# Forgetting attention: the third PSUM bank of the turned probabilities taken from another pool

## Chip, cores, metric

One Trainium2 chip, one of its cores. The metric is the device time of one execution in microseconds; the kernel before is given by the median of three runs. Every reading of the profile comes from one further, profiled execution.

The engines are called as in the profile: PE (TensorE, matrix products; PEld is its weight load), DVE (VectorE), ACT (ScalarE), POOL (GpSimd) and SP (SyncE, which only issues DMAs here). PE writes to PSUM, a memory of eight banks, each of 512 float32 values on each of 128 partitions; ACT and DVE read it from there.

## What is computed

One layer of a streaming encoder on 512 frames of 1024 channels, in float32. A combined projection of the normalised input feeds three branches: gated linear attention (GLA), forgetting attention with eight heads of 64 channels, and cross attention into 256 memory tokens. They are merged by gates, and a squared-ReLU MLP follows. The change lies in the forgetting attention:

```python
def forgetting_attention(q, k, v, log_f):
    F = jnp.cumsum(log_f, axis=1).transpose(0, 2, 1)
    ...
        s = jnp.einsum('bhqd,bhkd->bhqk', qi, kh) * scale
        s = s + Fi[..., None] - F[:, :, None, :]
        mask = k_pos[None, :] <= q_pos[:, None]
        p = jax.nn.softmax(jnp.where(mask, s, -jnp.inf), axis=-1)
        return jnp.einsum('bhqk,bhkd->bhqd', p.astype(vh.dtype), vh)
```

## The kernel before

**Precision and staging.** A float32 product is made of two or three reduced-precision ones: each operand is split into a high part (an ACT cast, `hi`, `PTh`, `whi`) and a low part (a DVE subtraction, `lo`, `PTl`, `wlo`), by `split` (L208 and L209) or `split_w` (L145 and L146), and `mm3` (L155 to L157) multiplies the parts. Weights come in chunks of 512 KB by SP's queue into `raw`, are split, and feed a projection `gT` (eight units of three matmuls of 512 columns, into one PSUM tile, which its `evac` empties).

**PSUM.** Two pools share the eight banks, four each. `mmt()` takes a tile of the pool `pmm`, meant for projections; `at_()` takes one of `pa`, meant for the attention steps. A tile's bank is free when the last instruction that reads the tile is done; the first matmul into the next tile of that bank waits for this.

**Order of the work.** PE's instructions run in the order in which the program text issues them. The order on the other engines is set at compile time by a scheduler that simulates the program; every engine runs its own list strictly in order.

**The stage of the change.** For each head h there are three steps:

- `fox_scores(h)`: adds the causal mask to a row of decays `nFb` (L515; `nFb` is fetched by a DMA from ACT's queue, L506), then for four query tiles takes a bank with `at_()`, makes two matmuls (L526, L527) of 256, 256, 384 and 512 columns, and empties the bank by one DVE instruction (L530), which also finds the row maximum; exponent (ACT, L532), reciprocal (L534) and scaling (L535) follow in `Pt`.
- `fox_turn(h)`: turns the lower triangle of the probabilities, ten blocks of 128 x 128, by PE transposes into three banks: `b0` (four blocks, L542), `b1` (four, L544 and L546) and `b2` (two, L549). Each bank is emptied by a split into `PTh` (ACT) and `PTl` (DVE): 512, 512 and 256 columns.
- `fox_values(h)`: takes one bank `po`, multiplies with the values (L558, L559), and adds the two halves of `po` (ACT copy `th` L563, DVE `oT` L567). After each odd head the pair's output is split into `ofh` and `ofl`.

`weave` strings these together as `fox_values(h-2)`, `fox_turn(h-1)`, `fox_scores(h)` for h from 1 to 9, as far as they exist, and puts units of projections in between, so that PE has work while ACT and DVE do the softmax. The 96 units are, in this order, `gla_k(0)` (8), `fox_pair(2)` (Q, then K: 16), `gla_k(1)` (8), `fox_pair(3)` (16), `gla_q(0)` and `gla_q(1)` (16), and the GLA values `gvg` (32). `gvg` opens four `pmm` tiles at once and holds them to the end of the stage. By the shares in `weave`, `fox_turn(0)` comes behind the end of the K projection of pair 1, `fox_turn(2)` one unit after the K projection of pair 2, `fox_turn(4)` two units after that of pair 3; `fox_turn(5)` comes at unit 62, two ahead of `gvg`.

A K projection is emptied by `k_evac` in two halves of 64 partitions: each an ACT cast and a DVE subtraction out of PSUM (`K`, L208 and L209) and an ACT copy to the other partitions (L497). A Q projection is emptied by `q_evac` in two halves (L490, L491 with the tile `tq`, L492).

So a head takes eight tiles of `pa`: one for `po`, three for the turn, four for the scores.

Of the kernel before, what the change touches and what calls it, by code (L numbers as in the profile page):

```python
# [64 lines left out]
def hybrid_block(ctx, tc, chunks, wst, memT, xN, cols, gffn, gfin, wup, cst, out):  # L65
# [6 lines left out]
    def nm(s):  # L72
        uid[0] += 1
        return f"{s}_{uid[0]}"
# [10 lines left out]
    def mmt(shape=None):  # L85
        return pmm.tile(shape or [P, 512], F32, tag="mm", name=nm("mm"))

    def at_(shape=None):
        return pa.tile(shape or [P, 512], F32, tag="a", name=nm("a"))
# [117 lines left out]
    def split(hi, lo, src):  # L207
        nc.scalar.copy(hi, src)  # L208
        return nc.vector.tensor_tensor(lo, src, f(hi), op=ALU.subtract).ins  # L209
# [41 lines left out]
    with pool("front") as fp:  # L251
# [101 lines left out]
        for k in range(KT):  # L353
# [3 lines left out]
            if k in (3, 5):  # L357
                h = k // 5
# [42 lines left out]
    with pool("fox") as xp:  # L401
# [135 lines left out]

        def fox_turn(h):
            Ps = live.pop(h)
            b0, b1, b2 = at_(), at_(), at_()  # L540
            for i in range(NT):
                nc.tensor.transpose(b0[:, i * P:(i + 1) * P], Ps[i][:, 0:P], ident)  # L542
            split(PTh[:, 0:512], PTl[:, 0:512], b0)
            nc.tensor.transpose(b1[:, 0:P], Ps[3][:, 3 * P:], ident)  # L544
            for i in range(1, NT):
                nc.tensor.transpose(b1[:, i * P:(i + 1) * P], Ps[i][:, P:2 * P], ident)  # L546
            split(PTh[:, 640:1152], PTl[:, 640:1152], b1)
            for i in range(2, NT):
                nc.tensor.transpose(b2[:, (i - 2) * P:(i - 1) * P], Ps[i][:, 2 * P:3 * P], ident)  # L549
            split(PTh[:, 1152:1408], PTl[:, 1152:1408], b2[:, :256])  # L550
# [53 lines left out]
        for h in range(1, 10):  # L604
            for fn, i, n in ((fox_values, h - 2, 3), (fox_turn, h - 1, 2), (fox_scores, h, 3)):
                if 0 <= i < 8:
                    steps.append(partial(fn, i))
                    shares.append(n)
# [882 lines left out]
```

## Time and profile before

| | us |
|---|---|
| median of 3 runs | 828.68 |
| lowest and highest | 828.56, 829.0 |
| the profiled execution's own time | 828.11 |
| its span, from the first to the last instruction | 826.3 |
| ACT busy in the span | 457.9 |
| POOL busy in the span | 104.8 |
| the forgetting attention's score matmuls (L526), first and last start | 77.1, 168.7 |

A row of the timeline or of the groups has start, duration, engine, line, operation, the tile written and the tiles read, and shapes. "[0.66 <-DVE PTl L209]" says that the engine was idle for 0.66 us ahead of this instruction, and that DVE's instruction at L209, which writes `PTl`, ended the wait. "x3" is three instructions in one row, whose duration runs from the start of the first to the end of the last. Successive instructions on one engine can overlap by a fraction, so PE's progress is read from the starts: two full projection matmuls start 0.23 us apart, though each is shown as 0.39 us long. Rows of stretches give start and end, length, and for each engine the busy time with the number of instructions, then the granted clock of PE, the DMA engines' busy share and GB/s. Rows of waits give the waiting engine, tile and line, what it waited for, the total in us, how often, and the longest.

### The profile page before, as it was taken

The page shows a single profiled execution, that of the slowest core. Times are in us where ns is not written, and L with a number is a line of the kernel's source. Part 1 is how long each engine was busy: PE and PEld are TensorE (multiplying, and loading weights), DVE is VectorE, ACT ScalarE, POOL GpSimd, SP SyncE. Part 2 cuts the span into 40 slices and gives each one's busy share as a digit, 9 for nine tenths or more (in the row PEclk, how much of TensorE's full clock was granted, in tenths as well). Part 3 has the DMA queues.
Part 4 walks back from the last instruction along what each step waited for, and adds up shares of the span by engine and source line. Part 5 has one row for each costly group of instructions (what it writes and reads, how often), then busy time and mean ns, then how long its engine had stood idle before and what let it go on. Part 6 is the DMA issues. An engine that isn't in the chain of part 4 may idle for free.

```text
span 826.3 us, 12441 instructions
## 1 busy us (share of the span) xinstructions
PE 813.3 (98%) x4759; PEld 715.4 (87%) x4759; DVE 603.3 (73%) x946; ACT 457.9 (55%) x717; POOL 104.8 (13%) x129
## 2 busy tenths in 40 slices
PE   8999999999999999999999999999999999999996
PEld 6788888888888888989999889988998899889984
DVE  5856887667545686885585647897689778887896
ACT  7765776653345233544354436774577367637764
POOL 1001100101102020132231100011001100110011
PEclk9999999999999999999999999999999999999999
DMA  9525666689687875677676513978757875896644
GB/s 331 183 102 162 185 191 192 190 209 297 146 264 230 229 223 157 128 185 190 151 200 171 178 51 112 275 171 207 237 197 155 229 228 170 191 235 205 164 81 129
DMA packets 39180, 155.60 MB, mean 188 GB/s; under 512 B 4880, under 2 KB 5840, under 8 KB 37072
## 3 DMA queue, kind: packets, MB, share of 16 engines
q1 hardware_dynamic: 27712, 95.54, 33.3%
q0 software_dynamic: 9328, 54.01, 31.7%
q10 hardware_dynamic: 2080, 5.26, 1.8%
q8 instruction: 37, 0.61, 0.3%
q14 instruction: 23, 0.19, 0.1%
HBM read 152.65 MB, written 31.49 MB: 223 GB/s over the span
## 4 chain that ended last, share of the span: by engine, by line
PE 91%; DVE 4%; DMA 2%; issue 1%; ACT 1%; POOL 0%; ACTq 0%; POOLq 0%; DVEq 0%
PE mm L155 23%; PE mm L156 23%; PE mm L157 23%; PE a L156 5%; PE a L155 5%; PE a L157 5%; PE a L797 1%; DMA xn<-in_xN_dram 1%; DMA memr<-in_memT_dram 1%; PE a L526 1%; PE a L559 1%; DVE wlo L146 1%; DVE h L1151 1%; PE a L558 1%; PE a L527 0%
## 5 line engine op out<-in xcount | busy, mean ns | idle before, releaser
L155 PE MATMUL mm<-uhi,whi 128*128 128x512 f32 (+1 forms) x352 | 126.1, 358 | 0.0
L157 PE MATMUL mm<-uhi,wlo 128*128 128x512 f32 (+1 forms) x352 | 123.8, 352 | 0.0
L156 PE MATMUL mm<-ulo,whi 128*128 128x512 f32 (+1 forms) x352 | 123.6, 351 | 0.0
L146 DVE TENSOR_TENSOR wlo<-raw,whi 128x1024 fp32r<-128x1024 f32 x68 | 88.0, 1298 | 43.3 <-ACT whi L145 42.9
L145 ACT CAST whi<-raw 128x1024 fp32r<-128x1024 f32 x68 | 71.3, 1049 | 78.9 <-PE mm L156 45.4
L1155 ACT CAST hi<-raw 128x1024 fp32r<-128x1024 f32 x65 | 68.2, 1049 | 49.6 <-PE mm L156 34.4
L1157 DVE TENSOR_TENSOR lo<-raw,hi 128x1024 fp32r<-128x1024 f32 x65 | 79.6, 1224 | 17.4 <-ACT hi L1155 17.4
L157 PEld LDWEIGHTS mm<-uhi,wlo 128*128 128x128 f32 x352 | 66.6, 189 | 9.1
L155 PEld LDWEIGHTS mm<-uhi,whi 128*128 128x128 f32 x352 | 66.7, 189 | 8.3 <-issue 0.3
L156 PEld LDWEIGHTS mm<-ulo,whi 128*128 128x128 f32 x352 | 66.7, 190 | 8.0
L1155 ACT CAST hi<-b 128x1024 fp32r<-128x1024 f32 x40 | 41.9, 1048 | 42.0 <-PE mm L157 24.0
L156 PE MATMUL mm<-u2l,hi 128*128 128x256 f32 x224 | 63.4, 283 | 0.0
L157 PE MATMUL mm<-u2h,lo 128*128 128x256 f32 x224 | 63.4, 283 | 0.0
L155 PE MATMUL mm<-u2h,hi 128*128 128x256 f32 x224 | 63.4, 283 | 0.0
L1341 POOL DMA_DIRECT2D b<-in_wst_dram x32 | 27.3, 853 | 271.3 <-DVE lo L1157 199.9
L1157 DVE TENSOR_TENSOR lo<-b,hi 128x1024 fp32r<-128x1024 f32 x40 | 48.9, 1224 | 14.1 <-ACT hi L1155 13.9
L156 PE MATMUL mm<-lo,ch 128*128 128x512 f32 x136 | 52.9, 389 | 0.0
L157 PE MATMUL mm<-hi,cl 128*128 128x512 f32 x136 | 52.9, 389 | 0.0
L155 PE MATMUL mm<-hi,ch 128*128 128x512 f32 x136 | 52.9, 389 | 0.0
L156 PE MATMUL mm<-u2sl,hi 128*128 128x256 f32 x168 | 47.6, 283 | 0.0
L157 PE MATMUL mm<-u2sh,lo 128*128 128x256 f32 x168 | 47.6, 283 | 0.0
L155 PE MATMUL mm<-u2sh,hi 128*128 128x256 f32 x168 | 47.6, 283 | 0.0
(401 smaller groups left out, 2159.9 us busy)
## 6 DMA issues: line engine op xcount, KB each, us to landing
raw<-in_wst_dram SPq DMA_DIRECT2D x114, 512.0 KB
b<-in_wst_dram POOLq DMA_DIRECT2D x32, 512.0 KB, 5.5
raw<-T SPq DMA_DIRECT2D x28, 512.0 KB
T<-in_wst_dram POOLq DMA_DIRECT2D x12, 1024.0 KB, 9.0
b<-in_wst_dram SPq DMA_DIRECT2D x16, 512.0 KB
wb<-in_wst_dram POOLq DMA_DIRECT2D x15, 512.0 KB, 5.5
wb<-in_wst_dram SPq DMA_DIRECT2D x8, 512.0 KB
T<-in_wst_dram POOLq DMA_DIRECT2D x6, 512.0 KB, 5.1
```

The source lines that it names most:

```text
L145: cast = nc.scalar.copy(hi, raw)
L146: low_now[0] = nc.vector.tensor_tensor(lo, raw, f(hi), op=ALU.subtract).ins
L155: nc.tensor.matmul(ps, lh, rh, start=start, stop=False, skip_group_check=on)
L156: nc.tensor.matmul(ps, lh, rl, start=False, stop=False, skip_group_check=on)
L157: nc.tensor.matmul(ps, ll, rh, start=False, stop=stop, skip_group_check=on)
L526: nc.tensor.matmul(ps[:, :w], q, K[e][:, 0, :w], start=True, stop=False)
L558: nc.tensor.matmul(po[:, q0:], vv, PTh[:, c0:c0 + w], start=n == 0, stop=False)
L559: nc.tensor.matmul(po[:, q0:], vv, PTl[:, c0:c0 + w], start=False, stop=n == 3)
L797: nc.tensor.matmul(ps[:, t, :], kk[:, sl], qq[:, sl], start=True, stop=True)
L1155: nc.scalar.copy(hi, raw)
L1157: nc.vector.tensor_tensor(lo, raw, f(hi), op=ALU.subtract)
L1341: nc.gpsimd.dma_start(to[i], wst[index["B", q, i, x]], accum_op=ALU.add)
```

## The change

In `fox_turn`, the bank `b2` comes from `pmm` for the heads 0 to 4, and from `pa` as before for the heads 5 to 7:

```diff
         def fox_turn(h):
             Ps = live.pop(h)
-            b0, b1, b2 = at_(), at_(), at_()
+            b0, b1, b2 = at_(), at_(), mmt() if h < 5 else at_()
             for i in range(NT):
                 nc.tensor.transpose(b0[:, i * P:(i + 1) * P], Ps[i][:, 0:P], ident)
```

(The conditional expression belongs to `b2` alone.) A head up to the fifth then takes seven tiles of `pa` and one of `pmm`.

## The prediction

> **What bounds the kernel now.** I read the page first: its busy times and the chain that ended last.
>
> ```profile
> span 826.3 us, 12441 instructions
> ## 1 busy us (share of the span) xinstructions
> PE 813.3 (98%) x4759; PEld 715.4 (87%) x4759; DVE 603.3 (73%) x946; ACT 457.9 (55%) x717; POOL 104.8 (13%) x129
> ...
> PE 91%; DVE 4%; DMA 2%; issue 1%; ACT 1%; POOL 0%; ACTq 0%; POOLq 0%; DVEq 0%
> ```
>
> PE stands idle for only 826.3 - 813.3 = 13.0 us, so a change outside PE's own work can win only part of those, and time won there reaches the end if PE stays the bound behind it. The view by stretches, asked for what lies behind the forgetting attention, says that it does:
>
> ```profile
> 185.00:500.00 315.00, 314.03 (x1838) 276.27 (x1837) 207.62 (x313) 129.98 (x203) 60.33 (x66) 1.00 0.67 184
> 500.00:802.00 302.00, 302.00 (x1940) 276.52 (x1939) 250.47 (x306) 192.26 (x259) 26.98 (x32) 1.00 0.72 194
> ```
>
> The columns are length, then PE, PEld, DVE, ACT, POOL. From 185 to 802 us PE lacks 0.97 us of 617, at a granted clock of 1.00. A microsecond gained before 185 us is therefore a microsecond at the end, unless something in those two stretches arrives at a fixed hour.
>
> Next I asked for the waits between 75 and 185 us. Of those of PE and its weight loads, one matters:
>
> ```profile
> PEld a L526 <- DVE PTl L209: 2.1, 5, 0.9
> ```
>
> L526 is a score matmul, L209 with PTl the DVE half of the split that empties a turned bank. A score group (eight matmuls, four banks) takes the four `pa` banks while `po`, `b0`, `b1` and `b2` of the step before are being given back. What the waits cost is read from four windows, each from the first score matmul to the first projection matmul behind the group; they are heads 1, 2, 3 and 5:
>
> ```profile
> 92.12:94.16 2.04, 1.83 (x10) 1.00 0.86 167
> 104.76:106.05 1.29, 1.29 (x9) 1.00 0.81 324
> 117.36:119.05 1.69, 1.60 (x10) 1.00 0.74 155
> 142.25:144.83 2.58, 1.83 (x9) 1.00 0.50 151
> ```
>
> Head 2 runs without a wait: 1.29 us. Heads 1, 3 and 5 lose 0.75, 0.40 and 1.29 us, 2.44 together; five waits are counted, two, one and two, so the other heads have none. **2.44 us is all that the change can take away directly.** These are the heads whose turn follows at once on the end of a K projection.
>
> **The change part by part.** It alters no operation: two transposes, one ACT cast and one DVE subtraction of 256 columns still go through the third bank. No DMA is added or moved, and PE's order is written out. What changes is which of the eight banks the third one is, for heads 0 to 4; the turns of heads 0, 2 and 4 stand ahead of the score groups of heads 1, 3 and 5.
>
> *The waits in head 5.* PE first, then DVE:
>
> ```profile
> 142.25 0.28 PE L526 MATMUL a<-K,Q 128*128 128x256 f32 x1
> 142.37 0.28 PE L527 MATMUL a<-K,Q 128*128 128x256 f32 x1
> 143.31 0.39 PE L526 MATMUL a<-K,Q 128*128 128x256 f32 x1 [0.66 <-DVE PTl L209]
> 143.53 0.28 PE L527 MATMUL a<-K,Q 128*128 128x256 f32 x1
> 143.91 0.45 PE L526 MATMUL a<-K,Q 128*128 128x384 f32 x1
> 144.19 0.34 PE L527 MATMUL a<-K,Q 128*128 128x384 f32 x1
> 144.37 0.40 PE L526 MATMUL a<-K,Q 128*128 128x512 f32 x1
> ```
>
> ```profile
> 139.44 0.76 DVE L515 TENSOR_TENSOR nFb<-nFb,cst_s 128x128 f32<-128x128 f32 x2 [2.22 <-DMA nFb<-dF]
> 140.12 0.68 DVE L209 TENSOR_TENSOR ofl<-oT,ofh 128x512 fp32r<-128x512 f32 x1
> 140.73 1.22 DVE L146 TENSOR_TENSOR wlo<-raw,whi 128x1024 fp32r<-128x1024 f32 x1
> 141.98 0.68 DVE L209 TENSOR_TENSOR K<-mm,K 64x512 fp32r<-64x512 f32 x1
> 142.58 0.67 DVE L209 TENSOR_TENSOR PTl<-a,PTh 128x512 fp32r<-128x512 f32 x1
> ```
>
> The same splits, cut off after the second and after the third:
>
> ```profile
> 142.58 1.27 DVE L209 TENSOR_TENSOR PTl<-a,PTh 128x512 fp32r<-128x512 f32 x2
> ```
>
> ```profile
> 142.58 1.60 DVE L209 TENSOR_TENSOR PTl<-a,PTh 128x512 fp32r<-128x512 f32 x3
> ```
>
> So `b0` comes free at 142.58 + 0.67 = 143.25, `b1` at 143.85, `b2` at 144.18. Tile 0 of the group takes `po`'s bank at once; tile 1 starts 0.06 behind `b0`, tile 2 0.06 behind `b1`. Tile 3 starts at 144.37, after `b2` is free: its wait is hidden behind tile 2's own matmuls.
>
> With the change one `pa` bank is spare. Tiles 0 and 1 start at once, tile 2 waits for `b0` (143.31), tile 3 for `b1` (143.91), nothing for `b2`. Tile 3 takes 144.83 - 144.37 = 0.46 us, and a tile that has waited about 0.10 more (first to second matmul of equal size 0.22 behind the wait, 0.12 without). The group ends at 143.91 + 0.10 + 0.46 = 144.47 in place of 144.83: **0.36 us saved**. The waits move one bank along rather than vanish, because the splits themselves come late.
>
> *Head 1*, the same way:
>
> ```profile
> 91.91 1.27 DVE L209 TENSOR_TENSOR PTl<-a,PTh 128x512 fp32r<-128x512 f32 x2
> ```
>
> ```profile
> 92.64 0.39 PE L526 MATMUL a<-K,Q 128*128 128x256 f32 x1
> 92.86 0.28 PE L527 MATMUL a<-K,Q 128*128 128x256 f32 x1
> 93.23 0.44 PE L526 MATMUL a<-K,Q 128*128 128x384 f32 x1
> ```
>
> `b1` is free at 93.18; tile 3 starts at 93.23 and the group ends at 93.23 + 0.56 = 93.79 in place of 94.16: **0.37 us**.
>
> *Head 3:*
>
> ```profile
> 116.81 1.60 DVE L209 TENSOR_TENSOR PTl<-a,PTh 128x512 fp32r<-128x512 f32 x3
> ```
>
> ```profile
> 118.13 0.44 PE L526 MATMUL a<-K,Q 128*128 128x384 f32 x1
> ```
>
> `b1` is free at 116.81 + 1.27 = 118.08. An unhindered tile 3 begins at 117.36 + (1.29 - 0.46) = 118.19. So no wait is left: **0.40 us**. The sum is 0.36 + 0.37 + 0.40 = **1.13 us**; bounds from these rows are 0 and 2.44.
>
> By the Trainium skill, "TensorE: Matmul & The Clock Gate", section "Back-to-back issue gap", a warm matmul takes a 2.4th of its columns in ns plus about 2.5, which would make a score group 2 x (109 + 109 + 163 + 216) ns = 1.19 us, the direct bound 2.74 and the best time 0.3 us lower. The trace's undisturbed group takes 1.29 us, and I keep that.
>
> *The added tile in the projections' pool.* At the first turn it meets two projection tiles that are still being emptied:
>
> ```profile
> 88.57 0.69 DVE L491 SCALAR_TENSOR_TENSOR tq<-mm,Q 64x512 fp32r<-64x512 f32 x1
> ```
>
> ```profile
> 89.83 0.27 PE L549 MATMUL a<-cst_s,Pt 128*128 128x128 f32 x1
> ```
>
> ```profile
> 94.18 0.69 DVE L209 TENSOR_TENSOR K<-mm,K 64x512 fp32r<-64x512 f32 x1
> ```
>
> Pair 1's Q tile is read until 89.26, its K tile until 94.87; the third turned bank is written from 89.83 and the next projection begins right behind. At most four are wanted at once, and four there are: cost 0. The cover is thin, 0.57 us from 89.26 to 89.83. Were `tq` put behind one 1.22 us `wlo`, PE would wait 0.65 us; at three such turns that is at most 1.95. The limit of five heads keeps turns 5 to 7, beside which the four GLA value tiles stand open, as they were: 0.
>
> *What goes on from there.* PE's earlier clock moves every later issue with it, with nothing added to a queue. The sum against the profiled execution: 828.11 (span 826.3 and 1.8 around it) - 1.13 = 826.98. That execution stands 0.57 below the median, so the time is 828.68 - 1.13 = 827.55, say **827.6 us**.
>
> **The rivals.** *B, the splits also come early.* In head 5 DVE runs without a gap from 139.44, when it got `nFb`. That row of decays was issued 6.4 us before; the one that held DVE two heads earlier landed in 3.7:
>
> ```profile
> 107.06 0.33 ACTq L506 DMA_DIRECT2D nFb<-dF  x1
> ```
>
> ```profile
> 110.77 0.76 DVE L515 TENSOR_TENSOR nFb<-nFb,cst_s 128x128 f32<-128x128 f32 x2 [0.79 <-DMA nFb<-dF]
> ```
>
> ```profile
> 133.04 0.33 ACTq L506 DMA_DIRECT2D nFb<-dF  x1
> ```
>
> If it lands 0.9 us sooner, or the compile-time scheduler, which puts DVE's order by its own simulation, sets the splits ahead of the 1.22 us `wlo`, head 5's remaining 0.93 us go too: 1.13 + 0.93 = 2.06, 826.6 us; with head 1's last 0.38, 826.2. For it: both are accidents of the present timing. Against: neither is what the change touches.
>
> *C, the gain is given back.* If `nFb` lands at the same hour while PE is 0.77 us ahead after heads 1 and 3, head 5's splits stay where they are and its group still ends at 144.47: 0.36 in all, 828.3 us. Against: the DMA's issue waits for work that moves ahead with PE.
>
> *D, slower: the K evacuation goes ahead of the turn.* Place: DVE and ACT at the three turns. Each pair's K tile is emptied in two halves; the second now comes behind the splits (94.18, in head 1). Between the halves ACT does this:
>
> ```profile
> 142.69 1.04 ACT L497 CAST K<-K 64x1024 fp32r<-64x1024 f32 x1 [1.55 <-DVE K L209]
> 143.75 0.58 ACT L208 CAST K<-mm 64x512 fp32r<-64x512 f32 x1
> ```
>
> If the new order has the second half finished first, the splits move back by 1.04 + 0.58 + 0.69 = 2.31 us, and tiles 2 and 3 with them. Delays of 0.37 us per head use up the gain; one head with the whole 2.31 gives -1.13 + 2.31 = +1.2, two give +3.5: 832.2 us. For it: K's tile now shares four banks with the turn, and its place already differs between heads. Against: nothing that the half needs comes earlier than before.
>
> *That the change does nothing* would need head 3's and head 5's first waits to be for ACT's or DVE's work rather than for banks; but the score operands are long there, and the waits end within 0.06 us of a split's end.
>
> **How the numbers follow.** The case of the sum has 45 in 100, its own range 826.7 to 828.3; B has 29 (826.6), C 9 (828.3), D 17 (832.2). About 0.2%, 1.66 us, is what a measurement of this kernel can tell from no change: faster means below 827.0, slower above 830.3. B and 13 of the sum's 45 are faster, 42; the other 32 and C are within, 41; D is slower, 17. The range runs from 825.9, a little under B's best, to 830.2, which takes in the 1.95 us of a late projection bank (829.5) and D at one head (829.9), and leaves out most of D and a little below.
>
> **What would show it.** In the changed profile the score groups of heads 1, 3 and 5 should last 1.67, 1.29 and 2.22 us, with tile 1 right behind tile 0, and tile 2 waiting where tile 1 did. The waits of weight loads for PTl should fall from five to four or fewer. No projection matmul should wait for a turned bank. B shows as a head 5 near 1.3 us and `nFb` landing sooner, C as head 5 with a longer wait, D as a K subtraction between `wlo` and PTl. I am wrong if the groups shorten as said and the time does not, or if PE gains idle time after 185 us.

## The result and the profile after

The changed kernel took 825.31 us (median of 6 runs, 824.98 to 826.39). The kernel before, beside it, took 828.50 (6 runs, 827.04 to 829.00). The ratio is 0.997, with a 95% interval of 0.996 to 0.998. Later, among the experiments, the same pair gave 826.20 and 828.15, ratio 0.9975 (0.9964 to 0.9986). The medians lie 3.19 and 1.95 us apart, so the change is worth 2 to 3 us, 1.7 to 2.8 times the 1.13 us of the sum. Taken by the ratio from the 828.68 us shown before, that is 826.2 us, inside the forecast range near its low end. That ratio is given to three digits only; the quotient of the two medians, 0.9961, would make it 825.5, and the median of 825.31 itself lies 0.6 us under the range.

The profiled execution of the changed kernel took 825.34 us. The top of its page and the line of its chain of waits:

```profile
span 823.5 us, 12442 instructions
...
PE 812.9 (99%) x4759; PEld 715.6 (87%) x4759; DVE 602.8 (73%) x946; ACT 457.7 (56%) x717; POOL 104.8 (13%) x129
...
PE 94%; DVE 2%; DMA 1%; issue 1%; ACT 1%; POOL 0%; ACTq 0%; POOLq 0%; DVEq 0%
```

The span is 2.8 us shorter, and PE's busy time is the same within 0.4 us: idle time went, not work. The stretches say where. The rows are the two stages behind the forgetting attention, then the score groups of heads 1, 2, 3 and 5, each from the first score matmul to the next projection matmul:

```profile
185.00:500.00 315.00, 314.94 (x1853) 277.57 (x1852) 207.13 (x313) 131.77 (x206) 60.34 (x66) 1.00 0.67 183
500.00:802.00 302.00, 302.00 (x1933) 276.19 (x1932) 252.09 (x307) 190.49 (x256) 27.87 (x33) 1.00 0.73 195
91.99:93.67 1.68, 1.68 (x9) 1.21 (x8) 1.68 (x6) 1.63 (x4) 0.00 (x0) 1.00 1.07 190
104.28:105.57 1.29, 1.29 (x10) 1.20 (x8) 0.86 (x5) 0.52 (x3) 0.00 (x0) 1.00 0.94 318
116.87:118.39 1.52, 1.52 (x10) 1.15 (x8) 1.52 (x6) 1.42 (x3) 0.00 (x0) 1.00 0.67 135
141.59:143.21 1.62, 1.62 (x9) 1.21 (x8) 1.59 (x6) 1.51 (x3) 0.00 (x0) 1.00 0.22 38
```

Two places gained. The score groups of heads 1, 3 and 5 went from 2.04, 1.69 and 2.58 us to 1.68, 1.52 and 1.62: 0.36 + 0.17 + 0.96 = 1.49 us. With 0.16 us of an earlier start, PE is 1.61 us ahead when head 7's group begins (166.42 for 168.03 us). And between 185 and 500 us, 210 us behind the change, PE lost 0.91 us of idle time: 314.03 busy became 314.94. The waits between 75 and 185 us fell as expected:

```profile
PEld a L526 <- DVE PTl L209: 0.9, 3, 0.3
```

The second place is the first `gate_group`. There the changed kernel has another order on DVE, although no line of `gate_group` changed. DVE, ACT and PE rows of the kernel before (`x` at L904 is the sum of which ACT casts `f2h` and DVE subtracts `f2l`, the operands of the next product; the two `ct` sums take an earlier product of the same gate into its results):

```profile
348.66 1.22 DVE L146 TENSOR_TENSOR wlo<-raw,whi 128x1024 fp32r<-128x1024 f32 x1
...
349.79 1.22 DVE L904 TENSOR_TENSOR x<-x,ulo 128x1024 f32<-128x1024 f32 x1
...
350.93 0.68 DVE L932 TENSOR_TENSOR ct<-ct,mm 128x512 f32<-128x512 f32 x1
351.10 1.05 ACT L905 CAST f2h<-x 128x1024 fp32r<-128x1024 f32 x1 [3.70 <-DVE x L904]
...
351.65 0.69 DVE L932 TENSOR_TENSOR ct<-ct,ct 128x512 f32<-128x512 f32 x1
...
352.21 0.38 PE L155 MATMUL mm<-f2h,whi 128*128 128x256 f32 x1
352.26 1.22 DVE L906 TENSOR_TENSOR f2l<-x,f2h 128x1024 fp32r<-128x1024 f32 x1
...
353.53 0.39 PE L156 MATMUL mm<-f2l,whi 128*128 128x256 f32 x1 [0.94 <-DVE f2l L906]
```

And of the changed kernel:

```profile
347.07 1.22 DVE L904 TENSOR_TENSOR x<-x,ulo 128x1024 f32<-128x1024 f32 x1
...
348.20 1.22 DVE L146 TENSOR_TENSOR wlo<-raw,whi 128x1024 fp32r<-128x1024 f32 x1
348.38 1.06 ACT L905 CAST f2h<-x 128x1024 fp32r<-128x1024 f32 x1 [2.37 <-DVE x L904]
...
349.46 1.23 DVE L906 TENSOR_TENSOR f2l<-x,f2h 128x1024 fp32r<-128x1024 f32 x1
...
350.41 0.28 PE L155 MATMUL mm<-f2h,whi 128*128 128x256 f32 x1
...
350.61 0.68 DVE L932 TENSOR_TENSOR ct<-ct,mm 128x512 f32<-128x512 f32 x1
...
350.75 0.39 PE L156 MATMUL mm<-f2l,whi 128*128 128x256 f32 x1
```

The sum of `x` now stands ahead of the 1.2 us split of `raw`, and `f2l` ahead of both `ct` sums. PE's 0.94 us wait is gone. Its matmul with `f2l` comes at 350.75 in place of 353.53, 2.78 us sooner, which is the whole gain of the span; 2.78 - 1.61 = 1.17 us of it arise here. That is a little more than the wait shown, for `f2h` was late too. The first matmul with `f2h` started 0.42 us behind the matmul ahead of it (351.79) in the kernel before and 0.23 us (350.18) in the changed one, and from there to the matmul with `f2l` it took 1.32 and 0.34 us: 0.19 + 0.98 = 1.17. The compiled programs differ in the order of their work only in a few places: this one (with ACT's `ct` copy, two places later), and DVE and ACT around the second half of a K projection in heads 1 and 3, which moved a little later.

### The profile page after: what moved, and what is told of

Read it like the earlier page. It is cut to its first block, busy times and chain, and to the rows that moved or that the text cites. A ratio compares the mean times of both kernels' runs of the same rounds, so it can differ in the third digit from the quotient of the medians.

```text
span 823.5 us, 12442 instructions
## 1 busy us (share of the span) xinstructions
PE 812.9 (99%) x4759; PEld 715.6 (87%) x4759; DVE 602.8 (73%) x946; ACT 457.7 (56%) x717; POOL 104.8 (13%) x129
## 4 chain that ended last, share of the span: by engine, by line
PE 94%; DVE 2%; DMA 1%; issue 1%; ACT 1%; POOL 0%; ACTq 0%; POOLq 0%; DVEq 0%
PE mm L155 23%; PE mm L156 23%; PE mm L157 23%; PE a L156 5%; PE a L155 5%; PE a L157 5%; PE a L797 1%; DMA xn<-in_xN_dram 1%; PE a L526 1%; DMA memr<-in_memT_dram 1%; PE a L559 1%; PE a L527 1%; PE a L558 1%; DVE h L1151 1%; DVE lo L1157 0%
```

## The experiments

Theory after this reading: the banks are worth about the sum, the new order in the gate group 1.17 us, and the two add. The runs were made in four sets, each on another chip and beside the kernel before, whose medians were 828.17 us in the first set (the first four rows), 828.15 in the second (the next four), 828.37 in the third (three rows) and 828.31 in the last (the last row). A gain is always taken against the kernel before of the same set.

| run | banks | gate order | median, us | ratio to before, 95% interval |
|---|---|---|---|---|
| `gate_order_only` | before | new | 827.02 | 0.9986 (0.9976 to 0.9996) |
| `gate_order_old` | changed | `f2l` late | 827.24 | 0.9987 (0.9977 to 0.9997) |
| `heads_0_2_4` | third, h = 0, 2, 4 | new | 826.21 | 0.9975 (0.9965 to 0.9985) |
| `heads_1_3` | third, h = 1, 3 | old | 828.59 | 1.0001 (0.9991 to 1.0011) |
| `changed_again` | changed | new | 826.20 | 0.9975 (0.9964 to 0.9986) |
| `first_bank` | first, h < 5 | old | 828.57 | 1.0004 (0.9996 to 1.0013) |
| `two_banks_and_order` | second and third, h = 0, 2, 4 | new | 825.30 | 0.9965 (0.9951 to 0.9978) |
| `decays_behind_splits` | before | old | 826.48 | 0.9979 (0.9970 to 0.9987) |
| `no_waits_left` | second and third, h = 0, 2, 4; decays moved | new | 824.53 | 0.9953 (0.9939 to 0.9966) |
| `splits_early_old_banks` | before, decays moved | new | 825.47 | 0.9962 (0.9949 to 0.9975) |
| `gate_f2l_only` | before | `f2l` early, sum late | 828.01 | 0.9996 (0.9987 to 1.0005) |
| `gate_sum_only` | before | sum early | 827.33 | 0.9987 (0.9978 to 0.9996) |

### Banks and gate order taken apart

`gate_order_only` keeps the kernel before's banks and writes the new order out: the split of `raw` is issued behind the sum of `x`, and the `ct` sums behind `f2l`.

```diff
-                nc.vector.tensor_tensor(xsum[1], xsum[1], block[1], op=ALU.add)
+                left_now[0] = nc.vector.tensor_tensor(xsum[1], xsum[1], block[1], op=ALU.add).ins
...
-                nc.vector.tensor_tensor(to[1], xsum[1], f(to[0]), op=ALU.subtract)
+                left_now[1] = nc.vector.tensor_tensor(to[1], xsum[1], f(to[0]), op=ALU.subtract).ins
...
+                with tc.issue_after(left_now[1]):
+                    take(6, p6)
...
-                p3 = product(3, split_w(block("22")))
+                with tc.issue_after(left_now[0]):
+                    w = split_w(block("22"))
+                p3 = product(3, w)
```

> The banks are those of the kernel before; only in the first gate group two dependences are written into the program, so that DVE makes the second subtraction of the left operand (L904) ahead of a weight split, and the low part of that operand (f2l) ahead of the two gate sums, as it does in the changed kernel. Theory (the change's second gain is a side effect of the compile-time order, 210 us behind the banks): the wait of the gate product for f2l, 0.94 us before, goes, and the time is 1.1 to 1.2 us below the kernel before: 827.3, with the score groups of heads 1, 3 and 5 as before (2.04, 1.69, about 2.6 us). Rival (the gain at the gate is only PE running ahead of its stage by what the banks gave): no gain, 828.5.

`gate_order_old` is the changed kernel with `f2l` issued behind both `ct` sums again.

```diff
-                    vec(c22, c22, c21, ALU.subtract)
+                    taken[0] = vec(c22, c22, c21, ALU.subtract)
...
-                nc.vector.tensor_tensor(to[1], xsum[1], f(to[0]), op=ALU.subtract)
+                with tc.issue_after(behind) if behind is not None else ExitStack():
+                    nc.vector.tensor_tensor(to[1], xsum[1], f(to[0]), op=ALU.subtract)
...
-                cast = lefts_2(S4, A12)
+                cast = lefts_2(S4, A12, taken[0])
```

> The banks are those of the changed kernel; one dependence in the first gate group puts DVE's two gate sums (0.68 and 0.69 us) ahead of f2l again. Theory (side effect of the order): f2l is 1.3 us later, the gate product waits again, and the time is about 1.2 us above the changed kernel: 826.5, 2.0 below the kernel before. Rival (the whole gain comes from the banks): 825.3, 3.2 below.

The order alone gave 828.17 - 827.02 = 1.15 us. The banks alone gave 828.17 - 827.24 = 0.93. Together, in `heads_0_2_4` and `changed_again`, they gave 1.96 and 1.95 beside a sum of 2.08: within the intervals they add. What `gate_order_old` missed of its expectation is size: its banks gave 0.93 us, not 2.0. The section on how much the banks give from run to run comes back to this.

### Which heads

One expression differs from the changed kernel in each: `mmt() if h in (0, 2, 4) else at_()`, and `mmt() if h in (1, 3) else at_()`.

> The third bank comes from the projections' pool for heads 0, 2 and 4 only. DVE's and ACT's orders are those of the changed kernel. Theory (only the score groups of heads 1, 3 and 5 had waits, and the turns ahead of them are those of heads 0, 2 and 4): the same as the changed kernel, 825.3. Rival (each borrowed bank gives its share): three fifths of 3.2 us, 826.6.

> The third bank comes from the projections' pool for heads 1 and 3 only; DVE's and ACT's orders are those of the kernel before. Theory (no score group behind these turns waited): no gain, 828.5. Rival (each borrowed bank gives its share): two fifths of 3.2 us, 827.2.

`heads_0_2_4` missed the 825.3 us that its theory took from the first comparison, and by the number alone, 1.96 us of gain, it fits the rival's three fifths of 3.2 us. What decides is that the changed kernel itself, run again below, gains the same 1.95 us, and that `heads_1_3` gains nothing. So heads 0, 2 and 4 hold all of the gain; the other two give nothing, for the groups behind them had no wait. `heads_1_3` also keeps the old order in the gate group, with its wait of 0.9 us, so a bank moved where nothing waits moved no order there either.

### How much the banks give from run to run

> The changed kernel once more, beside the kernel before on the chip of the other experiments. Theory (banks about -1.0 us, the new order in the first gate group about -1.15, the two add): 826.1 where the kernel before takes 828.2, ratio near 0.9975. Rival (banks and order together are worth the 3.2 us of the first comparison, because they help each other): 825.0, ratio near 0.996.

Measured 826.20, with the theory (on the chip of the second set). Heads 3 and 5 differ from the first profile of the same kernel, as two stretches of this run show:

```profile
117.56:118.84 1.28, 1.28 (x9) 1.16 (x8) 1.28 (x6) 1.18 (x3) 0.00 (x0) 1.00 1.24 256
142.05:144.40 2.35, 1.81 (x10) 1.21 (x9) 2.32 (x7) 1.69 (x3) 0.00 (x0) 1.00 0.46 139
```

Head 5's group took 2.35 us here and 1.62 there. The rows that explain it, of the first profile and then of this one, are the issue of head 5's decays, DVE's first instruction on them, and the splits behind that:

```profile
132.37 0.33 ACTq L506 DMA_DIRECT2D nFb<-dF  x1
...
138.19 0.76 DVE L515 TENSOR_TENSOR nFb<-nFb,cst_s 128x128 f32<-128x128 f32 x2 [1.63 <-DMA nFb<-dF]
...
141.32 1.27 DVE L209 TENSOR_TENSOR PTl<-a,PTh 128x512 fp32r<-128x512 f32 x2
```

```profile
132.84 0.33 ACTq L506 DMA_DIRECT2D nFb<-dF  x1
...
139.36 0.76 DVE L515 TENSOR_TENSOR nFb<-nFb,cst_s 128x128 f32<-128x128 f32 x2 [2.34 <-DMA nFb<-dF]
...
142.50 1.27 DVE L209 TENSOR_TENSOR PTl<-a,PTh 128x512 fp32r<-128x512 f32 x2
```

DVE's first instruction on the decays starts 5.82 us after their issue in the one and 6.52 us after it in the other. I call this time the landing, since the DMA ended DVE's wait in both. The same two starts and head 5's group, from the timelines of the runs that leave head 5's decays where they were and move no other bank than the third:

| third bank at turn 4 | run | issue to DVE's start, us | head 5's group, us |
|---|---|---|---|
| `pmm` | first profile of the changed kernel | 5.82 | 1.62 |
| `pmm` | `gate_order_old` | 5.99 | 1.81 |
| `pmm` | `heads_0_2_4` | 6.44 | 2.25 |
| `pmm` | `changed_again` | 6.52 | 2.35 |
| `pa` | `heads_1_3` | 6.07 | 2.23 |
| `pa` | `gate_order_only` | 6.32 | 2.49 |
| `pa` | kernel before | 6.40 | 2.58 |
| `pa` | `gate_f2l_only` | 6.52 | 2.70 |
| `pa` | `gate_sum_only` | 6.57 | 2.74 |

Within either kind of bank the group lengthens one for one with the landing. At the same landing, 6.52 us, the bank is worth 2.70 - 2.35 = 0.35 us. The rest of head 5's gain in the first profile, 0.96 - 0.36 = 0.60, goes with the early landing in that execution (6.40 - 5.82 = 0.58). In the same nine runs head 1 is 1.68 us with the changed bank and 2.02 to 2.05 with the old one. Head 3 averages 1.36 with it (1.52, 1.30, 1.34, 1.28) and 1.72 without (1.69, 1.76, 1.41, 1.92, 1.82). So the banks give 0.36 + 0.36 + 0.35 = 1.07 us.

Head 3 follows the landing of its own decays too. With the old bank its group is 1.41 us at a landing of 3.44 us (`gate_order_only`), 1.69 at 3.71 (the kernel before) and 1.92 at 3.92 (`gate_f2l_only`). With the changed one it is 1.34 at 3.71 (`heads_0_2_4`), so the bank is worth 0.35 us there, and 1.52 at 3.88 in the first profile, which lost some 0.18 us by that later landing.

### Which bank

`first_bank` takes `b0` in place of `b2` from `pmm`: `b0, b1, b2 = mmt() if h < 5 else at_(), at_(), at_()`.

> The turn's first bank instead of its third from the projections' pool, for the same five heads. Theory (tile 2 of a score group now takes the second turned bank and tile 3 the third, each at the same moment as in the kernel before, so only the wait of the tile that stood behind the first bank goes, and the group ends where it ended): no gain in the fox stage, score groups of heads 1, 3 and 5 as in the kernel before (about 2.0, 1.7 and 2.6 us); 828.2 if the order of the first gate group is the old one. Rival (any one bank more is what counts, whichever it is): the same gain as with the third bank, about 1.0 us less, 827.2.

828.57 us: no gain, as the theory had it. In head 5 the second tile no longer waits, and the third then waits for `b1` and the group ends no sooner:

```profile
143.08 0.28 PE L526 MATMUL a<-K,Q 128*128 128x256 f32 x1
143.20 0.28 PE L527 MATMUL a<-K,Q 128*128 128x256 f32 x1
144.47 0.44 PE L526 MATMUL a<-K,Q 128*128 128x384 f32 x1 [0.99 <-DVE PTl L209]
```

Its group is 2.54 us, from 142.85 to 145.39. One bank more is not what counts, but that the last wait is for an earlier split. This run has the old gate order too, with the same number of tiles from `pmm` as the changed kernel.

### Taking the waits away altogether

`two_banks_and_order` takes `b1` and `b2` from `pmm` for heads 0, 2 and 4, with the gate order of `gate_order_only`; against the kernel before, the line of the banks is:

```diff
-            b0, b1, b2 = at_(), at_(), at_()
+            b0, b1, b2 = at_(), *(mmt() if h in (0, 2, 4) else at_() for _ in range(2))
```

> Second and third turned bank from the projections' pool for heads 0, 2 and 4, and the changed kernel's order of VectorE in the first gate group written out. Theory (only tile 3 of a score group can still wait, for the first turned bank, which is free 0.6 us before the second): score groups of heads 1, 3 and 5 at 1.3 to 1.5 us, 0.4 to 0.9 us below the changed kernel's sum, 825.4 where the changed kernel takes 826.1. Rival (the projection that follows the turn then waits for a bank of its own pool, about 0.65 us at each of three turns): 826.5 to 828, and a wait of the first projection matmul behind each turn.

825.30: 0.9 us under `changed_again` at the median, at the theory's upper end, though the intervals overlap. Its six runs lie in two lots, three at 824.20 to 824.22 us and three at 826.39 to 827.52, with none near the median, so the size of this gain rests on the groups. Heads 1, 3 and 5 took 1.29, 1.28 and 1.56 us, and no PE wait in front of a projection shows.

`decays_behind_splits` leaves the banks alone and moves the mask sums on the decays, so that DVE does not stand ahead of the splits waiting for the DMA:

```diff
-        live = {}
+        live, turned = {}, [None]
...
-                nc.vector.tensor_tensor(nFb[:, b, :], nFb[:, b, :], m, op=ALU.add)
+                with tc.issue_after(turned[0]) if h else ExitStack():
+                    nc.vector.tensor_tensor(nFb[:, b, :], nFb[:, b, :], m, op=ALU.add)
...
-            split(PTh[:, 1152:1408], PTl[:, 1152:1408], b2[:, :256])
+            turned[0] = split(PTh[:, 1152:1408], PTl[:, 1152:1408], b2[:, :256])
```

> The kernel before's banks; the two mask sums on the decays (L515) are issued behind the turn's third split, so that VectorE does not stand still for the row of decays ahead of the splits. Theory (head 5's late splits come from VectorE's wait for that row): head 5's score group falls from 2.6 to about 1.7 us, the others stay, 0.6 to 0.9 us below the kernel before, 827.4, if the decays are not then late for the step that reads them. Rival (the splits are late through the splits of the weights and the K evacuation ahead of them): head 5 stays at 2.6 and the time at 828.2 or above.

826.48, 1.67 us below the kernel before, nearly twice the most that I expected. DVE around head 5:

```profile
138.68 1.22 DVE L146 TENSOR_TENSOR wlo<-raw,whi 128x1024 fp32r<-128x1024 f32 x1 [0.26 <-ACT whi L145]
139.94 0.68 DVE L209 TENSOR_TENSOR K<-mm,K 64x512 fp32r<-64x512 f32 x1
140.55 1.60 DVE L209 TENSOR_TENSOR PTl<-a,PTh 128x512 fp32r<-128x512 f32 x3
142.07 0.74 DVE L516 TENSOR_TENSOR nFb<-nFb,cst_s 128x128 f32<-128x128 f32 x2
```

The splits begin at 140.55 for 142.58 us, and the decays have landed when DVE comes to them (no idle time in that row). Heads 3 and 5 are at 1.31 and 1.29 us, so this gained 0.38 + 1.29 = 1.67 without one bank more; head 1 stays at 2.04, since there the splits wait behind weight and K work, not behind decays. I had expected 1.7 us in head 5: I reckoned with a part of the DMA's wait, and the move also brought head 3's splits forward. Here too the compiled order changed beside the edit: in head 5, for one, DVE takes the second half of the K projection (142.85 us) ahead of the group's first L530 and no longer behind it. So the run shows the move with the order that came of it.

`no_waits_left` joins all three edits; `splits_early_old_banks` is that with the kernel before's banks.

> All three together: second and third turned bank from the projections' pool for heads 0, 2 and 4, the mask sums on the decays behind the turn's third split, and the changed kernel's order in the first gate group written out. Theory (the only losses are the three late score groups, 2.44 us in the kernel before, and the late f2l, 1.2 us): all four score groups at 1.3 us, no wait for f2l, 3.4 to 3.6 us below the kernel before, 824.7. Rival (the row of decays, now summed later, is late for the step that reads it, or the two banks are missed by a projection): 825.5 or more, with a wait of PE behind L530 or in front of a projection.

> The same with the kernel before's banks: only the mask sums are moved and the order in the gate group is the changed kernel's. Theory (a bank more only covers splits that come late; with the splits early the banks are worth only what head 1 and 3 still wait): heads 1 and 3 keep up to 0.75 and 0.4 us of wait unless the move also brings their splits forward, head 5 is near 1.7 us; about 1.5 + 1.15 = 2.6 below the kernel before, 825.5, that is 0.8 above the kernel with all three. Rival (banks are worth their 1.0 us whatever the splits do): 1.0 to 1.5 us above the kernel with all three.

824.53 and 825.47 us, 0.94 apart where the theory said 0.8. The stretches of heads 1, 2, 3 and 5 in `no_waits_left`:

```profile
92.10:93.39 1.29, 1.29 (x10) 1.20 (x9) 1.29 (x3) 1.26 (x3) 0.00 (x0) 1.00 0.76 133
104.01:105.30 1.29, 1.29 (x10) 1.20 (x8) 0.96 (x4) 0.43 (x2) 0.00 (x0) 1.00 0.85 286
116.60:117.89 1.29, 1.29 (x9) 1.20 (x8) 1.29 (x4) 0.82 (x2) 0.00 (x0) 1.00 1.02 203
141.11:142.40 1.29, 1.29 (x10) 1.20 (x8) 1.26 (x4) 0.55 (x1) 0.00 (x0) 1.00 0.08 16
```

The whole direct bound of 2.44 us is reached. It is the fastest kernel of the study: 0.9953 (0.9939 to 0.9966) of the kernel before.

### What in the gate order counts

The two moves of `gate_order_only`, one at a time. `gate_f2l_only` keeps only `take(6, p6)` behind `f2l`:

> The kernel before's banks and, in the first gate group, one thing alone: the subtraction that makes f2l (L906) is issued ahead of the two ct sums (L932), while the sum of x (L904) stays behind the split of raw. Theory (the two sums of 0.68 us each ahead of f2l are what made PE wait 0.94 us): f2l is ready 1.36 us sooner, the wait is gone, 0.9 to 1.1 us below the kernel before, 827.2. Rival (the place of L904 ahead of the 1.2 us split counts as much): f2h comes no sooner, PE then waits there or at f2l for about half, 0.4 to 0.6 us below, 827.7.

828.01: no gain that can be told, and the theory fell. DVE does come to `f2l` sooner, and then stands idle:

```profile
349.87 1.22 DVE L904 TENSOR_TENSOR x<-x,ulo 128x1024 f32<-128x1024 f32 x1
...
351.18 1.05 ACT L905 CAST f2h<-x 128x1024 fp32r<-128x1024 f32 x1 [3.66 <-DVE x L904]
...
352.26 1.23 DVE L906 TENSOR_TENSOR f2l<-x,f2h 128x1024 fp32r<-128x1024 f32 x1 [1.17 <-ACT f2h L905]
...
353.55 0.39 PE L156 MATMUL mm<-f2l,whi 128*128 128x256 f32 x1 [0.88 <-DVE f2l L906]
```

In the kernel before the `ct` sums had only filled that time. `gate_sum_only` keeps the other move, the split of `raw` behind the sum of `x`; one `ct` sum then stands ahead of `f2l`:

> The kernel before's banks and, in the first gate group, the other half of the new order alone: the sum of x (L904) is issued ahead of the 1.22 us split of raw; one ct sum (L932) stands ahead of f2l (L906), the other behind it. gate_f2l_only showed that f2l, put ahead of both ct sums, still starts at 352.26 us, since it waits for f2h and that for L904. Theory (two chains make f2l late: L904 behind the split, then f2h and f2l; and the ct sums in front of f2l; both must go): VectorE does L904 at 348.66, the split at 349.79, a ct sum at 350.93, f2l from 351.6 to 352.8, so PE's wait falls from 0.94 to about 0.3 us and the kernel takes 0.6 to 0.8 us less than before, 827.5 where that takes 828.2. Rival (the place of L904 is all): the wait is gone, 1.1 to 1.2 us less, 827.0. Second rival (the place of neither alone does anything): the wait stays at 0.9 and the time at 828.2.

```profile
348.71 1.22 DVE L904 TENSOR_TENSOR x<-x,ulo 128x1024 f32<-128x1024 f32 x1
349.84 1.22 DVE L146 TENSOR_TENSOR wlo<-raw,whi 128x1024 fp32r<-128x1024 f32 x1
...
350.98 0.68 DVE L932 TENSOR_TENSOR ct<-ct,mm 128x512 f32<-128x512 f32 x1
351.57 1.22 DVE L906 TENSOR_TENSOR f2l<-x,f2h 128x1024 fp32r<-128x1024 f32 x1
...
352.85 0.39 PE L156 MATMUL mm<-f2l,whi 128*128 128x256 f32 x1 [0.51 <-DVE f2l L906]
```

827.33 us, 0.98 below; in the trace 0.72 of the 1.17 us arise in this group, and 0.51 us of wait stay, behind the one `ct` sum. `gate_order_old` is the fourth case: its sum of `x` stands early, but with both `ct` sums ahead of `f2l` PE loses as much as ever. From its last matmul ahead of `f2h` to the one with `f2l` it takes 1.76 us, where the kernel before takes 1.74 and the changed one 0.57:

```profile
350.02 0.68 DVE L933 TENSOR_TENSOR ct<-ct,mm 128x512 f32<-128x512 f32 x1
350.74 0.69 DVE L933 TENSOR_TENSOR ct<-ct,ct 128x512 f32<-128x512 f32 x1
...
351.35 1.22 DVE L907 TENSOR_TENSOR f2l<-x,f2h 128x1024 fp32r<-128x1024 f32 x1
...
352.63 0.39 PE L156 MATMUL mm<-f2l,whi 128*128 128x256 f32 x1 [1.25 <-DVE f2l L907]
```

So two chains of nearly equal length made `f2l` late, and removing either alone leaves the other: `f2l` early behind a late sum gives nothing, an early sum with both `ct` sums ahead of `f2l` nothing either, with one of them 0.72 us, and both moves whole 1.17 us.

## Why the prediction was partly right

*What bounds the kernel* held. The time won in the score groups was still there at 350 us and at the end of the span. But I read "from 185 to 802 us PE lacks 0.97 us" as a sign that nothing happens there, and did not ask what that 0.97 was: nearly all of it was one wait, PE's 0.94 us for `f2l`, and it could go.

*The sum of the banks* held. Head 1 was forecast at 1.67 us and is 1.68; head 3 at 1.29, and is 1.28 to 1.52; head 5 at 2.22 for the landing of the profile before, 6.40 us, and is 2.25 at 6.44. Head 3 at the landing of the profile before, 3.71 us, is 1.34: the prediction had no wait left there, and 0.05 us were. The 0.36 + 0.37 + 0.40 = 1.13 us measure 1.07 over the runs, and the change alone gave 0.93 at the median with the gate order undone. That waits move one bank along rather than vanish is what `first_bank` shows most plainly.

*The added tile* costs nothing, as put at 0. At the first turn of the changed kernel the `tq` that empties the Q tile, the turn's third bank (now `mm`) and the projection behind it:

```profile
88.56 0.69 DVE L491 SCALAR_TENSOR_TENSOR tq<-mm,Q 64x512 fp32r<-64x512 f32 x1
...
89.70 0.38 PE L549 MATMUL mm<-cst_s,Pt 128*128 128x128 f32 x2
89.83 0.48 PE L155 MATMUL mm<-uhi,whi 128*128 128x512 f32 x1
```

`tq` ends at 89.25, 0.45 us ahead of L549, and the projection follows at once. Two tiles at each turn, in `two_banks_and_order`, were no dearer.

*What goes on from there* is the step that failed: "PE's earlier clock moves every later issue with it, with nothing added to a queue". Nothing was added, but DVE's queue was put in another order, 210 us behind the edit. This 1.17 us is what the sum lacks: 1.07 + 1.17 = 2.24. The second comparison gave 1.95 us. The first gave 3.19, and the 0.95 us above the sum are not settled: in its one profile 0.16 us are an earlier start and 0.42 the landings of the decays (0.60 gained in head 5, 0.18 lost in head 3), and its other executions were not profiled. I had named the scheduler in rival B, but looked for its effect only in the stage of the change. Why it chose another order is not settled. `first_bank`, with as many tiles from `pmm` but no earlier score groups, keeps the old one, which would suit a scheduler whose simulated PE came earlier; its simulation was not looked into.

That a gain of about twice the sum still lies in the forecast range is luck: the low end of the range was set for rival B, and the gate order, which no case of the prediction had, took the time near it.

*Rival B* was half seen, in the first profile. There head 5's decays did land sooner and its splits came early, but the change does not bring that with it: in `changed_again`, the same kernel, the landing was 6.52 us. What made it early is open. *Rival C* did not happen: the issue of the decays went from 133.04 to 132.37, 0.67 us earlier, as PE's turn did. *Rival D* did not either: the second K half stayed behind the splits, and in heads 1 and 3 moved a little further back (94.18 to 94.44 us in head 1). *That the change does nothing* is out by `gate_order_old` and by the groups.

## What to carry to other kernels

Where an order is made at compile time, an edit can change it far from its place: compare the order of every engine's instructions, and give the order its own run, before the gain is put down to the edit. A small idle remainder in a stage that looks full should be read to its row, for it is what such a change can win or lose. And a wait for a buffer is cured at its source or moved: one bank more gave 1.07 us, a DMA's wait taken out of the queue ahead of the splits gave 1.67 without any.

## What the runs showed of the hardware

The same 512 KB fetch of decays, issued at the same place in the program, reached DVE in 5.82 to 6.57 us, and a score group followed it one for one: a spread of 0.75 us out of one transfer. What sets the landing was not looked into. The head of the program varies more: head 0's first score matmul, with the same PE program ahead of it, started between 76.92 us (`gate_f2l_only`) and 78.91 us (`two_banks_and_order`). A single pair of profiles is therefore compared by the lengths of its stages, not by its span; the 2.8 us between the first two spans held 0.16 us of start and 0.42 of landings, both of which vary between executions without the change.
